# State space matrices of both halves built beside the first conditioning, both scans ahead of the readouts

## The chip, the cores and the metric

The kernel runs on one core of a Trainium2 chip. The metric is the device time of one execution in microseconds. TensorE (PE) multiplies matrices, VectorE (DVE), ScalarE (ACT) and GpSimd (POOL) do the rest, and SyncE (SP) issues the transfers. TensorE's clock has two levels, 1.2 and 2.4 GHz; the profile tells the granted level as a share of the upper one.

## What is computed

Two layers of a diffusion transformer with 512 latent tokens and 256 context tokens, D = 1024. Each layer mixes three things in parallel: windowed attention, a short convolution, and a bidirectional state space model (SSM) of 16 groups; then an MLP. The conditioning vector gives shifts, scales and gates. The context is computed in layer 0 only, beyond what layer 1 reads of it. The part that the change touches:

```python
mod = (c_act @ w_ada[l] + b_ada[l])[:, None, :]             # conditioning
q, k, v, cb, cc, cx, u = split_in_proj(h_lat @ w_in)
conv = cb * centred_conv3(cc * cx, conv_w)

lam_bar = jnp.exp(lam * dt)                                  # SSM, per direction and group
b_bar = ((lam_bar - 1) / lam)[..., None] * lax.complex(b_re, b_im)
# drive(t, d) = einsum('blgi,gpi->blgp', t, b_bar[d])
h_lat_f = diag_scan(lam_bar[0], drive(u, 0), h_ctx_f[:, -1], False)
h_lat_b = diag_scan(lam_bar[1], drive(u, 1), h_ctx_b[:, 0], True)
y = real(einsum('blgp,gip->blgi', hf, c_mat[0]) + einsum('blgp,gip->blgi', hb, c_mat[1])) + d_skip * t
g = gelu(y); out = g * sigmoid(g @ w_glu + b_glu)
```

## The kernel before

**Stages.** For each layer `block` runs `phase_w` (conditioning, SSM, convolution), `phase_a` (attention, the SSM's gate, output projection) and the MLP. In layer 0 `startup` comes first: the first half of the conditioning, the SSM's input projection u and the SSM matrices. The order on the engines is not that of the code: a scheduler places every instruction by dependences, buffers and its own times, and the code's order is what it starts from. Large products are made in three matmuls of high and low parts (L638 to L640). The conditioning that is left is spread over `phase_w` in slices (`step(sn[i])`), whose 32-row matmuls stand at L754 and whose weights SP loads in blocks of 512 KB (`w` from `w_ada`); ACT and DVE or POOL split each loaded weight into its two parts (L622, L623).

**The SSM.** Tokens are taken in chunks of 8, so that 96 chunks remain (64 of them latent). The 16 groups are worked in two halves of 8, and each in two directions. Its functions, by half:
- `ssm_mats`: input matrices `x` (DVE, L334 to L340), transposed on PE (L346) and copied to `xt`; small matmuls of 32 columns (L356 to L366, 24 of them) for the kernel strips, copied by ACT to `ssm_k` and stored to DRAM (`strips`). In the text these are the strip matmuls.
- `ssm_tm`: SP loads the strips back in Toeplitz form (`ssm_tr`, 512 KB) and ACT copies them into the order that the readout needs (`ssm_tm`, L568 through a helper).
- `ssm_out_mat`: the matrices `ssm_o` that lead from the state to the output (DVE, L442 to L447, 6 rows per direction).
- `ssm_scan`: the drive matmuls (L462), thirteen DVE instructions with the scan itself (L471 to L498, L484 the scan) per direction, which leave the states `ssm_s`; in layer 0 it calls `ssm_out_mat` for each direction.
- `ssm_read`: for each of four pairs of groups, one Toeplitz matmul per group (L519) and four of the states per group (L525), each on one half of PE's rows; the two groups of a pair go to two PSUM banks (`ps_s`). ACT and DVE evict each bank (L532 to L535) and SP stores it to `y_d`.

In layer 1 the matrices of both halves were made in layer 0's MLP and spilled to DRAM (`ssm_spill`); `ssm_fill` loads them.

**The convolution.** `conv("cc")`, `conv("cx")` and `conv("cb")` are projections into the PSUM tag `ps_m` of four banks; cc is evicted by ACT (L1127), cx and cb by DVE (L1129, L1142, L1144).

**Pools.** The tag A4 has four buffers of 4 KB per partition for `ssm_x`, `ssm_s` and `ssm_tr`; `ssm_tm` has one buffer of its own; the general pool `f4` has 19 buffers of 4 KB.

**Order in the code of `phase_w`.** Layer 0: matrices and Toeplitz matrix of half 0 come from `startup`; then scan 0, matrices of half 1, readout 0, conv cc, scan 1, Toeplitz 1, conv cx, readout 1, conv cb. Layer 1: scan 0, fill 1, scan 1, conv cc, readout 0, Toeplitz 1, conv cx, readout 1, conv cb. After that `phase_a` starts with the kv projection.

Of the kernel before, what the change touches and what calls it, by code (L numbers as in the profile page):

```python
# [7 lines left out]
F32 = mybir.dt.float32  # L8
# [7 lines left out]
P = 128  # L16
# [361 lines left out]

def ssm_tm(E, l, half):

    tr = E.mp.tile([P, 8, 8, 16], F32, name="ssm_tr", tag="A4", bufs=E.na4)
    tm = E.mp.tile([P, 8, 8, 16], F32, name="ssm_tm", tag="ssm_tm", bufs=1)
    st = E.strips[l]
    E.bdma(tr.rearrange("p t g i -> p t (g i)"),
           bass.AP(tensor=st.tensor, offset=st.offset + half * P, ap=[[256, P], [4096, 8], [1, P]]))
    E.copy(tm, tr.rearrange("p t g i -> p g t i"))
    return tm
# [27 lines left out]
def ssm_fill(E, half):  # L415
    U = {}
    for d in range(2):
        u = U[d] = Env()
        c0 = (2 + d) * 8 + half * 4
        u.cs = slice(c0, c0 + 4)  # L420
        u.xt = E.mp.tile([P, 2, 4, P], F32, name="ssm_xt", tag="B4", bufs=E.nb4)
        E.bdma(u.xt.rearrange("p q k c -> p (q k c)"), E.sp_x[half, d])
    for d in range(2):
        U[d].o = E.mp.tile([P, 2, 4, 8, 16], F32, name="ssm_o", tag="B4", bufs=E.nb4)
        E.bdma(U[d].o.rearrange("p q k t i -> p (q k t i)"), E.sp_o[half, d])
    return U


def ssm_out_mat(E, S, u, half, d):

    nc = E.nc
    V, G = nc.vector, nc.gpsimd
    cs = u.cs
    sl = slice(1, 9) if d == 0 else slice(8, 0, -1)
    pr, pi = bc(E.pw[:, 0, cs, sl], 3, 16), bc(E.pw[:, 1, cs, sl], 3, 16)
    pn = slice(half * 64, half * 64 + 64)
    cr = bc(S.c[:, 0, d, pn].rearrange("p (a i) -> p a i", i=16), 2, 8)
    ci = bc(S.c[:, 1, d, pn].rearrange("p (a i) -> p a i", i=16), 2, 8)
    o = E.mp.tile([P, 2, 4, 8, 16], F32, name="ssm_o", tag="B4", bufs=E.nb4)
    t1 = E.mp.tile([P, 4, 8, 16], F32, name="ssm_m", tag="T3", bufs=2)  # L440
    t2 = E.mp.tile([P, 4, 8, 16], F32, name="ssm_m", tag="T3", bufs=2)
    V.tensor_mul(o[:, 0], pr, cr)  # L442
    V.tensor_mul(t1, pi, ci)
    V.tensor_add(o[:, 0], o[:, 0], t1)
    V.tensor_mul(o[:, 1], pr, ci)
    V.tensor_mul(t2, pi, cr)
    V.tensor_sub(o[:, 1], o[:, 1], t2)  # L447
    u.o = o


def ssm_scan(E, S, U, u_t, l, half, lat_only):
    nc = E.nc
    V, G = nc.vector, nc.gpsimd
    sp = {}
    for d in range(2):
        u = U[d]
# [28 lines left out]
        s = E.mp.tile([P, 2, 4, NCH + CCH], F32, name="ssm_s", tag="A4", bufs=E.na4)  # L485
# [13 lines left out]
        if d == 1 and not lat_only:  # L499
            nc.scalar.copy(s[:, :, :, 0:CCH], s[:, :, :, NCH:NCH + CCH])  # L500
        sp[d] = s
        if l == 0:
            ssm_out_mat(E, S, u, half, d)
    return sp


# [455 lines left out]
def block(E, l, cols):  # L962
    tc, nc, a = E.tc, E.nc, E.a
    with psum_phase(E, f"w{l}", s=3, a=1, m=4) as E.pp, \
            tc.tile_pool(name=f"ssm{l}", bufs=1, reuse_waits="tile") as E.mp:
        E.ps, E.na4, E.nb4 = 's', 4, 4
        E.xa = lambda shape: E.mp.tile(shape, F32, name="ssm_x", tag="A4", bufs=E.na4)
        E.wpool = False
        if l == 0:
            cols = startup(E)  # L970
        st = phase_w(E, l, cols)
    with psum_phase(E, f"a{l}", m=2, t=2, q=2) as E.pp, \
            tc.tile_pool(name=f"att{l}", bufs=1, reuse_waits="tile") as E.ap:
        E.wpool = True
        phase_a(E, l, cols, st)
    with psum_phase(E, f"m{l}", m=3, a=1, q=2) as E.pp, \
            tc.tile_pool(name=f"mlp{l}", bufs=1, reuse_waits="tile") as E.g4p, \
            tc.tile_pool(name=f"prep{l}", bufs=1, reuse_waits="tile") as E.mp:
        E.ps, E.nb4 = 'a', 2
        E.xa = E.f4  # L980
        a2 = phase_post(E, l, st)
        return phase_mlp(E, l, a2)
# [7 lines left out]
def startup(E):  # L990
# [38 lines left out]
    S = E.S = ssm_load(E, a, 0)  # L1029
    S.tab = E.mp.tile([P, 2, 16, NCH], F32, name="ssm_tab", tag="ssm_tab", bufs=1)  # L1030
    ssm_table(E, 0, 16, S.tab)
    E.U0 = ssm_mats(E, E.S, 0, 0), ssm_tm(E, 0, 0)
    return cols


# [41 lines left out]
def phase_w(E, l, cols):  # L1077
    nc, a, tc = E.nc, E.a, E.tc
    V, G = nc.vector, nc.gpsimd
    both = l == 0  # L1080
# [11 lines left out]
    def step(n):  # L1092
        for _ in range(n):
            next(ada, None)
# [9 lines left out]
    S = E.S if l == 0 else Env()  # L1104
    if l == 1:
        S.tab = E.mp.tile([P, 2, 16, NCH], F32, name="ssm_tab", tag="ssm_tab", bufs=1)
        U0, t0 = ssm_fill(E, 0), ssm_tm(E, 1, 0)
        E.bdma(S.tab, E.sp_t)
    else:
        U0, t0 = E.U0  # L1110
    for h in range(2):
        E.bdma(u_t[h], E.u_d[h].rearrange("t i g c -> (t i) g c"))
    zs, mC = {}, {}
# [35 lines left out]
    step(sn[1])  # L1149
    wcx = blocks(E, wc, 4, 2, 8)  # L1150
    step(sn[2])
    s0 = ssm_scan(E, S, U0, u_t, l, 0, not both)
    if both:
        U1 = ssm_mats(E, S, 0, 1)
        ssm_read(E, U0, t0, s0, u_t, 0, y_d, not both)
        conv("cc", wcc)
        s1 = ssm_scan(E, S, U1, u_t, l, 1, not both)
    else:
        U1 = ssm_fill(E, 1)
        s1 = ssm_scan(E, S, U1, u_t, l, 1, not both)  # L1160
        conv("cc", wcc)
        ssm_read(E, U0, t0, s0, u_t, 0, y_d, not both)
    t1 = ssm_tm(E, l, 1)
    wcb = blocks(E, wc, 0, 2, 8)
    step(sn[3])
    conv("cx", wcx)
    ssm_read(E, U1, t1, s1, u_t, 1, y_d, not both)
    step(sn[4])
    conv("cb", wcb)
    st = Env()  # L1170
# [343 lines left out]
```

## Time and profile before

| | |
|---|---|
| median of 3 runs | 1687.18 us (1686.0 to 1687.56) |
| the profiled execution | 1684.55 us |
| its span in the profile | 1682.8 us |
| mean granted clock | 0.958 |
| PE busy | 1575.2 us, 94% |
| DVE busy | 891.2 us, 53% |
| ACT busy | 554.5 us, 33% |
| POOL busy | 302.9 us, 18% |

The span is the time from the first to the last instruction of the profiled execution, and its own time is 1.75 us longer. A row of busy time says how long an engine had an instruction in work, not how fast: at the lower clock PE is just as busy. A matmul of fp32 operands (L346, L462, L519, L525) shows as two records, so "x16" of these lines is 8 instructions.

### The profile page before, as it was taken

What the parts mean: (1) busy time and instruction counts of PE and PEld (TensorE: products, weight loads), DVE (VectorE), ACT (ScalarE), POOL (GpSimd) and SP (SyncE); (2) the same over time, 40 slices, a digit from 0 to 9 for tenths busy, and PEclk for the clock granted to TensorE, in tenths of its full rate; (3) what the DMA queues carried; (4) which work ended last, traced back from release to release, by engine and by line L of the source; (5) the groups of instructions that cost most, each with busy time, mean ns of one, the idle gap of its engine ahead of it and who ended that gap; (6) DMA issues with size and microseconds to landing.
All of it is one profiled execution on the core that took longest, in us unless ns stands there. A gap on an engine that the chain in (4) does not pass through costs nothing.

```text
span 1682.8 us, 22623 instructions
## 1 busy us (share of the span) xinstructions
PE 1575.2 (94%) x8872; PEld 1274.2 (76%) x8872; DVE 891.2 (53%) x1982; ACT 554.5 (33%) x1041; POOL 302.9 (18%) x231
## 2 busy tenths in 40 slices
PE   5999698999999999999999997999889899999997
PEld 2777576667888888868688875788667788888885
DVE  7882627766885463323333367643774733333335
ACT  5421125554523122121312344122554522322232
POOL 0000122002312111011111126012102322222222
PEclk9997699999999999999999998959999899999999
DMA  9564212004133222072621245822302232222223
GB/s 342 190 207 157 98 48 76 1 20 175 71 135 106 80 100 76 25 274 68 237 72 51 88 151 193 313 83 64 113 1 99 77 101 99 100 100 100 89 99 125
DMA packets 73274, 193.80 MB, mean 115 GB/s; under 512 B 15184, under 2 KB 25680, under 8 KB 73040
## 3 DMA queue, kind: packets, MB, share of 16 engines
q1 hardware_dynamic: 73168, 192.37, 33.1%
q8 instruction: 69, 1.13, 0.3%
q14 instruction: 37, 0.30, 0.1%
HBM read 172.15 MB, written 20.19 MB: 114 GB/s over the span
## 4 chain that ended last, share of the span: by engine, by line
PE 78%; DVE 13%; ACT 4%; DMA 2%; issue 2%; POOL 1%; DVEq 0%; SPq 0%; ACTq 0%; POOLq 0%
PE ps_m L638 14%; PE ps_m L639 14%; PE ps_m L640 14%; PE ps_q L639 8%; PE ps_q L638 8%; PE ps_q L640 8%; PE ps_s L525 2%; PE ps_a L754 2%; ACT p L873 2%; DVE p L865 1%; PE ps_t L898 1%; DVE p L878 1%; PE ps_s L519 1%; DVE w L623 1%; PE ps_t L891 1%
## 5 line engine op out<-in xcount | busy, mean ns | idle before, releaser
L622 ACT CAST w<-w 128x1024 fp32r<-128x1024 f32 x172 | 178.8, 1049 | 477.2 <-PE ps_q L639 312.8
L623 POOL TENSOR_TENSOR w<-w 128x1024 fp32r<-128x1024 f32 x79 | 193.2, 2445 | 780.1 <-ACT w L622 343.5
L638 PE MATMUL ps_q<-w,f 128*128 128x512 f32 x640 | 247.3, 391 | 3.4 <-DVE g L1466 2.6
L639 PE MATMUL ps_q<-w,f 128*128 128x512 f32 x640 | 248.5, 390 | 1.9 <-DVE w L623 1.1
L640 PE MATMUL ps_q<-w,f 128*128 128x512 f32 x640 | 246.7, 389 | 0.0
L623 DVE TENSOR_TENSOR w<-w 128x1024 fp32r<-128x1024 f32 x93 | 117.8, 1266 | 149.7 <-ACT w L622 125.3
L638 PE MATMUL ps_m<-g,w 128*128 128x256 f32 (+1 forms) x544 | 178.8, 333 | 2.3 <-DVE g L711 1.8
L639 PE MATMUL ps_m<-g,w 128*128 128x256 f32 (+1 forms) x544 | 179.7, 332 | 0.0
L640 PE MATMUL ps_m<-g,w 128*128 128x256 f32 (+1 forms) x544 | 177.9, 331 | 0.0
L639 PE MATMUL ps_m<-f,w 128*128 128x512 f32 (+1 forms) x464 | 171.6, 371 | 0.5 <-POOL f L714 0.3
L640 PE MATMUL ps_m<-f,w 128*128 128x512 f32 (+1 forms) x464 | 171.2, 370 | 0.0
L638 PE MATMUL ps_m<-f,w 128*128 128x512 f32 (+1 forms) x464 | 169.5, 369 | 0.3 <-DVE f L1071 0.3
L1472 DVE TENSOR_TENSOR g<-g,ps_q 128x1024 f32<-128x1024 f32 x60 | 73.3, 1221 | 178.6 <-PE ps_q L640 178.6
L638 PEld LDWEIGHTS ps_q<-w,f 128*128 128x128 f32 x640 | 119.8, 188 | 29.9 <-DVE g L1466 3.9
L639 PEld LDWEIGHTS ps_q<-w,f 128*128 128x128 f32 x640 | 120.2, 188 | 27.5 <-DVE w L623 2.0
L640 PEld LDWEIGHTS ps_q<-w,f 128*128 128x128 f32 x640 | 120.2, 188 | 24.7
L638 PE MATMUL ps_m<-w,f 128*128 128x512 f32 (+1 forms) x336 | 124.6, 374 | 6.8 <-DVE p L918 4.0
L640 PE MATMUL ps_m<-w,f 128*128 128x512 f32 (+1 forms) x336 | 124.2, 371 | 0.0
L639 PE MATMUL ps_m<-w,f 128*128 128x512 f32 (+1 forms) x336 | 123.0, 368 | 0.0
L1395 DVE SCALAR_TENSOR_TENSOR relu<-ps_m,relu 128x512 f32<-128x512 f32 (+1 forms) x104 | 58.7, 566 | 120.0 <-ACT relu L1394 119.8
L638 PEld LDWEIGHTS ps_m<-g,w 128*128 128x128 f32 x544 | 104.0, 193 | 15.7 <-issue 2.5
L639 PEld LDWEIGHTS ps_m<-g,w 128*128 128x128 f32 x544 | 104.9, 193 | 11.6 <-issue 1.6
(284 smaller groups left out, 2578.7 us busy)
## 6 DMA issues: line engine op xcount, KB each, us to landing
w<-in_w_ada SPq DMA_DIRECT2D x88, 512.0 KB
w<-in_w_mlp_in SPq DMA_DIRECT2D x64, 512.0 KB
w<-in_w_mlp_out SPq DMA_DIRECT2D x64, 512.0 KB
w<-in_w_out SPq DMA_DIRECT2D x16, 512.0 KB
w<-in_w_conv SPq DMA_DIRECT2D x12, 512.0 KB
h_d<-g SPq DMA_DIRECT2D x12, 512.0 KB
w<-in_w_q SPq DMA_DIRECT2D x8, 512.0 KB
f<-h_d SPq DMA_DIRECT2D x8, 512.0 KB
```

Source lines behind the costliest of these rows:

```text
L519: nc.tensor.matmul(out(g), tm[:, g8].rearrange("p t i -> p (t i)"), u_t[half][:, g8, lo:NCH], start=True, stop=False, skip_group_check=True)
L525: nc.tensor.matmul(out(g), U[d].o[rows, q, k].rearrange("p t i -> p (t i)"), sp[d][rows, q, k, lo:NCH], start=False, stop=d == 1 and q == ...
L622: nc.scalar.copy(hi, raw)
L623: (nc.gpsimd if turn % 2 and E.wpool else nc.vector).tensor_sub(lo, raw, hi.bitcast(F32))
L638: nc.tensor.matmul(out, lh, rh, start=first, stop=False)
L639: nc.tensor.matmul(out, lh, rl, start=False, stop=False)
L640: nc.tensor.matmul(out, ll, rh, start=False, stop=last)
L754: nc.tensor.matmul(pa[32 * b:32 * b + 32, k * 256:(k + 1) * 256], E.cT[:, kc], raw[k][:, b * 256:(b + 1) * 256], start=kc == 0 and k == 0, ...
L865: V.tensor_tensor_reduce(out=p[i][:, :nk * P], in0=pq[:, l0:768], in1=E.mask[:, moff:moff + nk].rearrange("p a b -> p (a b)"), scale=0.125 ...
L873: nc.scalar.activation(p[i][:, :nk * P], p[i][:, :nk * P], AF.Exp, bias=nm[:, i:i + 1], accum_out=sm[:, i:i + 1])
L1395: V.scalar_tensor_tensor(out=s, in0=pt, scalar=0.0, in1=s, op0=OP.max, op1=OP.mult)
L1472: V.tensor_add(facc[t], facc[t], pq)
```

## The change

Both Toeplitz tiles come from the pool `f4`; A4 has five buffers in place of four. `startup` makes the matrices of both halves, and no Toeplitz matrix. `ssm_scan` no longer makes the out matrices. In `phase_w` Toeplitz 0 comes ahead of scan 0, and the code's order is then: scan 0, out matrices of half 0 (layer 0) or fill 1 (layer 1), scan 1, readout 0, Toeplitz 1, out matrices of half 1 (layer 0), conv cc, readout 1, conv cx, conv cb.

```diff
@@ -378,8 +378,7 @@
 
 def ssm_tm(E, l, half):
 
-    tr = E.mp.tile([P, 8, 8, 16], F32, name="ssm_tr", tag="A4", bufs=E.na4)
-    tm = E.mp.tile([P, 8, 8, 16], F32, name="ssm_tm", tag="ssm_tm", bufs=1)
+    tr, tm = (E.f4([P, 8, 8, 16]) for _ in range(2))
     st = E.strips[l]
     E.bdma(tr.rearrange("p t g i -> p t (g i)"),
            bass.AP(tensor=st.tensor, offset=st.offset + half * P, ap=[[256, P], [4096, 8], [1, P]]))
@@ -499,8 +498,6 @@
         if d == 1 and not lat_only:
             nc.scalar.copy(s[:, :, :, 0:CCH], s[:, :, :, NCH:NCH + CCH])
         sp[d] = s
-        if l == 0:
-            ssm_out_mat(E, S, u, half, d)
     return sp
 
 
@@ -963,7 +960,7 @@
     tc, nc, a = E.tc, E.nc, E.a
     with psum_phase(E, f"w{l}", s=3, a=1, m=4) as E.pp, \
             tc.tile_pool(name=f"ssm{l}", bufs=1, reuse_waits="tile") as E.mp:
-        E.ps, E.na4, E.nb4 = 's', 4, 4
+        E.ps, E.na4, E.nb4 = 's', 5, 4
         E.xa = lambda shape: E.mp.tile(shape, F32, name="ssm_x", tag="A4", bufs=E.na4)
         E.wpool = False
         if l == 0:
@@ -1029,7 +1026,7 @@
     S = E.S = ssm_load(E, a, 0)
     S.tab = E.mp.tile([P, 2, 16, NCH], F32, name="ssm_tab", tag="ssm_tab", bufs=1)
     ssm_table(E, 0, 16, S.tab)
-    E.U0 = ssm_mats(E, E.S, 0, 0), ssm_tm(E, 0, 0)
+    E.U = [ssm_mats(E, S, 0, h) for h in range(2)]
     return cols
 
 
@@ -1104,10 +1101,10 @@
     S = E.S if l == 0 else Env()
     if l == 1:
         S.tab = E.mp.tile([P, 2, 16, NCH], F32, name="ssm_tab", tag="ssm_tab", bufs=1)
-        U0, t0 = ssm_fill(E, 0), ssm_tm(E, 1, 0)
+        U = [ssm_fill(E, 0)]
         E.bdma(S.tab, E.sp_t)
     else:
-        U0, t0 = E.U0
+        U = E.U
     for h in range(2):
         E.bdma(u_t[h], E.u_d[h].rearrange("t i g c -> (t i) g c"))
     zs, mC = {}, {}
@@ -1149,22 +1146,24 @@
     step(sn[1])
     wcx = blocks(E, wc, 4, 2, 8)
     step(sn[2])
-    s0 = ssm_scan(E, S, U0, u_t, l, 0, not both)
+    tms = [ssm_tm(E, l, 0)]
+    sp = [ssm_scan(E, S, U[0], u_t, l, 0, not both)]
     if both:
-        U1 = ssm_mats(E, S, 0, 1)
-        ssm_read(E, U0, t0, s0, u_t, 0, y_d, not both)
-        conv("cc", wcc)
-        s1 = ssm_scan(E, S, U1, u_t, l, 1, not both)
+        for d in range(2):
+            ssm_out_mat(E, S, U[0][d], 0, d)
     else:
-        U1 = ssm_fill(E, 1)
-        s1 = ssm_scan(E, S, U1, u_t, l, 1, not both)
-        conv("cc", wcc)
-        ssm_read(E, U0, t0, s0, u_t, 0, y_d, not both)
-    t1 = ssm_tm(E, l, 1)
+        U.append(ssm_fill(E, 1))
+    sp.append(ssm_scan(E, S, U[1], u_t, l, 1, not both))
+    ssm_read(E, U[0], tms[0], sp[0], u_t, 0, y_d, not both)
+    tms.append(ssm_tm(E, l, 1))
+    if both:
+        for d in range(2):
+            ssm_out_mat(E, S, U[1][d], 1, d)
+    conv("cc", wcc)
     wcb = blocks(E, wc, 0, 2, 8)
     step(sn[3])
+    ssm_read(E, U[1], tms[1], sp[1], u_t, 1, y_d, not both)
     conv("cx", wcx)
-    ssm_read(E, U1, t1, s1, u_t, 1, y_d, not both)
     step(sn[4])
     conv("cb", wcb)
     st = Env()
```

Above line 500 the new kernel's line numbers are lower by 1, and from 501 on by 3: L525 becomes L522, L1127 becomes L1124.

What the scheduler makes of it, at three places of layer 0. On ACT, near the end of the strip matmuls, before: `f4_1309` and `f4_1363` are conv cc's tiles, `ssm_k` the strips, `ssm_tm_994` the Toeplitz matrix of half 0.

```order
L1127 COPY f4_1309<-ps_m_1337 128x256
L568 COPY ssm_xt_925<-ps_s_926 128x512
L568 COPY ssm_xt_925<-ps_s_932 128x512
L1127 COPY f4_1363<-ps_m_1365 128x512
L568 COPY ssm_xt_947<-ps_s_948 128x512
L568 COPY ssm_xt_947<-ps_s_954 128x512
L568 COPY ssm_k_977<-ps_s_960 128x128
L568 COPY ssm_k_990<-ps_s_981 128x128
L622 CAST w_1520<-w_1516 128x1024
```

The same place on ACT now: `f4_1155` and `f4_1387` are the Toeplitz matrices of half 0 and half 1, `f4_1386` the load of the second, `f4_1408` and `f4_1462` conv cc's tiles.

```order
L565 COPY f4_1155<-f4_1154 128x1024
L619 CAST w_1524<-w_1518 128x1024
L565 COPY ssm_k_1060<-ps_s_1043 128x128
L565 COPY ssm_k_1073<-ps_s_1064 128x128
L565 COPY f4_1387<-f4_1386 128x1024
L1124 COPY f4_1408<-ps_m_1410 128x512
L1124 COPY f4_1408<-ps_m_1436 128x256
L1124 COPY f4_1462<-ps_m_1464 128x512
L1124 COPY f4_1462<-ps_m_1490 128x256
```

The four evictions of conv cc now stand behind the second half's strips and its Toeplitz copy, before they stood ahead of them.

On PE, in the first readout of layer 0, before: `ps_s_1253` and `ps_s_1254` are its two banks, `ssm_s` the states, `ssm_o` the out matrices.

```order
L519 MATMUL ps_s_1253<-u_t0_998,ssm_tm_994 128x96
L519 MATMUL ps_s_1254<-u_t0_998,ssm_tm_994 128x96
L525 MATMUL ps_s_1253<-ssm_s_1106,ssm_o_1113 128x96
L525 MATMUL ps_s_1254<-ssm_s_1106,ssm_o_1113 128x96
L525 MATMUL ps_s_1253<-ssm_s_1106,ssm_o_1113 128x96
L525 MATMUL ps_s_1254<-ssm_s_1106,ssm_o_1113 128x96
L525 MATMUL ps_s_1253<-ssm_s_1153,ssm_o_1161 128x96
L525 MATMUL ps_s_1254<-ssm_s_1153,ssm_o_1161 128x96
```

The first readout now: `ps_s_1330` is its first bank.

```order
L516 MATMUL ps_s_1330<-u_t0_1077,f4_1155 128x96
L522 MATMUL ps_s_1330<-ssm_s_1189,ssm_o_1235 128x96 x2
L522 MATMUL ps_s_1330<-ssm_s_1227,ssm_o_1244 128x96 x2
L516 MATMUL ps_s_1330<-u_t0_1077,f4_1155 128x96
L522 MATMUL ps_s_1330<-ssm_s_1189,ssm_o_1235 128x96 x2
L522 MATMUL ps_s_1330<-ssm_s_1227,ssm_o_1244 128x96 x2
```

The groups of the two banks took turns before; now the four groups of one bank follow each other, and those of the other (`ps_s_1331`) come after 4 transposes (L763) and 31 matmuls of projections (24 of 256 columns, 7 of 512).

On DVE, at the end of `phase_w` in layer 0, before: the second scan's last direction (`ssm_z_1482`) and its out matrix (`ssm_o_1503`), then the evictions of the second readout (L533, L535).

```order
L484 SCALAR_TENSOR_TENSOR ssm_z_1482<-ssm_rz_1490,ssm_z_1482 128x384 x2
L495 TENSOR_TENSOR ssm_s_1495<-ssm_z_1482,ssm_tab_850 128x8x95
L496 TENSOR_TENSOR ssm_zt_1496<-ssm_z_1482,ssm_tab_850 128x8x95
L443 TENSOR_TENSOR ssm_m_1504<-ssm_pw_84,ssm_c_835 128x512
L497 TENSOR_TENSOR ssm_s_1495<-ssm_s_1495,ssm_zt_1496 128x4x95
L498 TENSOR_TENSOR ssm_s_1495<-ssm_s_1495,ssm_zt_1496 128x4x95
L444 TENSOR_TENSOR ssm_o_1503<-ssm_o_1503,ssm_m_1504 128x512
L446 TENSOR_TENSOR ssm_m_1505<-ssm_pw_84,ssm_c_835 128x512
L447 TENSOR_TENSOR ssm_o_1503<-ssm_o_1503,ssm_m_1505 128x512
L533 SCALAR_TENSOR_TENSOR ssm_y2_1774<-ssm_y2_1774,ps_s_1732 128x384
```

The end of the second half's out matrices on DVE now: `ssm_o_1390` and `ssm_o_1399` are those of its two directions, `ssm_y2_1379` and `ssm_gl_1380` belong to the first readout's second bank, `ssm_y2_1656` to the second readout.

```order
L530 SCALAR_TENSOR_TENSOR ssm_y2_1379<-ssm_y2_1379,ps_s_1331 128x384
L442 TENSOR_TENSOR ssm_m_1400<-ssm_pw_84,ssm_c_835 128x512
L446 TENSOR_TENSOR ssm_o_1390<-ssm_o_1390,ssm_m_1392 128x512
L443 TENSOR_TENSOR ssm_o_1399<-ssm_o_1399,ssm_m_1400 128x512
L445 TENSOR_TENSOR ssm_m_1401<-ssm_pw_84,ssm_c_835 128x512
L532 SCALAR_TENSOR_TENSOR ssm_gl_1380<-ssm_y2_1379,ps_s_1331 128x384
L446 TENSOR_TENSOR ssm_o_1399<-ssm_o_1399,ssm_m_1401 128x512
L530 SCALAR_TENSOR_TENSOR ssm_y2_1656<-ssm_y2_1656,ps_s_1614 128x384
```

The second half's scan and out matrices, which came after the first readout and most of the convolution, are now done beside the first readout.

## Rows read from the trace of the kernel before

**Rows 1.** The page's busy line: busy us, share of the span, instructions.

```profile
PE 1575.2 (94%) x8872; PEld 1274.2 (76%) x8872; DVE 891.2 (53%) x1982; ACT 554.5 (33%) x1041; POOL 302.9 (18%) x231
```

**Rows 2.** Windows of layer 0: length, busy us by engine, PE clock, DMA share, GB/s.

```profile
80.00:90.00 10.00, 10.00 (x101) 7.37 (x101) 1.68 (x3) 3.19 (x9) 0.62 (x3) 0.83 0.60 234
...
130.00:140.00 10.00, 10.00 (x84) 7.39 (x83) 0.28 (x1) 2.02 (x4) 0.11 (x1) 0.89 0.62 202
140.00:150.00 10.00, 10.00 (x54) 8.80 (x55) 0.00 (x0) 0.27 (x1) 0.11 (x1) 0.50 0.07 25
150.00:160.00 10.00, 9.86 (x96) 7.01 (x93) 3.52 (x6) 1.96 (x3) 0.00 (x0) 0.59 0.35 106
160.00:170.00 10.00, 9.77 (x123) 6.73 (x124) 7.52 (x14) 1.63 (x3) 0.10 (x1) 1.00 0.98 336
170.00:180.00 10.00, 4.90 (x30) 3.98 (x28) 10.00 (x15) 4.59 (x5) 5.24 (x2) 0.77 0.37 125
180.00:190.00 10.00, 1.46 (x7) 0.97 (x6) 9.85 (x19) 0.41 (x1) 0.30 (x2) 0.50 0.28 106
```

**Rows 3.** Waits of PE from 72 to 202: us in total, times, longest.

```profile
PE ps_s L525 <- DVE ssm_o L444: 11.5, 2, 7.0
PE ps_s L525 <- DVE ssm_o L447: 2.0, 2, 1.6
PE ps_s L519 <- DVE ssm_z L473: 0.6, 1, 0.6
```

**Rows 4.** Chain of waits, 138 to 159: start, us, what (first readout, Toeplitz load).

```profile
148.47 1.10 PE ps_s L519 x4
149.57 1.96 PE ps_s L525 x16
...
153.82 4.10 DMA ssm_tr<-strips
```

**Rows 5.** Chain of waits in layer 1's first readout, groups one by one.

```profile
1094.34 1.03 PE ps_s L525 x8
1095.37 0.36 PE ps_s L519 x2
...
1099.12 0.62 PE ps_s L519 x2
1099.74 1.90 PE ps_s L525 x8
```

**Rows 6.** Windows behind the two readouts: length, PE busy us, clock, DMA share, GB/s.

```profile
154.60:158.10 3.50, 3.50 (x36) 0.50 0.54 157
...
201.20:206.00 4.80, 4.80 (x23) 0.50 0.16 41
```

**Rows 7.** Timeline of ACT: start, us, instruction, idle before it and what ended that.

```profile
69.96 0.60 ACT L1127 COPY f<-ps_m 128x512 f32<-128x512 f32 x1
...
92.44 1.05 ACT L568 COPY ssm_tm<-ssm_tr 128x1024 f32<-128x1024 f32 x1 [1.53 <-DMA ssm_tr<-strips]
```

**Rows 8.** Prices on PE from the chain, in four stretches of 64 to 97.

```profile
64.39 0.23 PE ps_m L639
...
69.50 0.12 PE ps_m L638
...
78.97 0.56 PE ps_a L754 x4
...
86.03 0.22 PE ps_s L358 x2
...
95.32 0.81 PE ps_s L462 x16
```

**Rows 9.** Chain of waits at the operand split, 60 to 62.

```profile
59.88 0.60 DVE ssm_x L338
```

**Rows 10.** Waits of PE in layer 1, 1090 to 1140.

```profile
PE ps_s L519 <- ACT ssm_tm L568: 3.3, 1, 3.3
```

**Rows 11.** VectorE's groups from 155 to 193: busy us, mean ns, idle before.

```profile
L623 DVE TENSOR_TENSOR w<-w 128x1024 fp32r<-128x1024 f32 x2 | 4.1, 2058 | 0.0
```

## The prediction

> **What bounds the kernel now.** I read the page's busy line first: PE has 94% of the span [rows 1], so a gain can only come from stretches where PE waits, or where it works at the lower clock. The windows of 10 us over layer 0's projections come next [rows 2]: PE is full up to 170, has 4.90 and 1.46 busy us in the next two windows, and the granted clock is 0.50 from 140 to 150 and from 180 to 190. That is the place of the change. The list of waits says who is late there [rows 3]: PE waits for VectorE's `ssm_o` rows, 11.5 + 2.0 us, and 0.6 us for `ssm_z`, 14.1 in all. The chain of waits around 140 to 160 shows what else is slow: the first readout runs at the low clock, a pair of groups costing 1.10 + 1.96 = 3.06 us, and the second half's Toeplitz load takes 4.10 us [rows 4]. In layer 1 the same views show readouts group by group [rows 5], and one wait of 3.3 us for `ssm_tm` [rows 10]. The rest, some 1500 us, the change leaves alone but for small reorderings.
>
> The profiled execution took 1684.55 us (span 1682.8), the median of the three runs is 1687.18; I sum against the profiled one and add the 2.63 between them at the end. Below, "low" is a granted clock of 0.50, 1.2 GHz, and "full" is 1.00, 2.4 GHz.
>
> **The idle time (layer 0): -14.1 us.** Before, the second half's scan and out matrices stand on VectorE behind the conv rows, so PE gets to the second readout before its operands. After, both scans stand in front, and the last `ssm_o` row is row 381 of VectorE, ahead of the second readout's first eviction. Does it fit? From 160 to 190 VectorE is busy 7.52 + 10.00 + 9.85 = 27.4 us; from 130 to 160 it is idle for 9.72 + 10.00 + 6.48 = 26.2 us [rows 2]. Of the 27.4, 4.1 are two weight splits [rows 11] that don't move, and conv and conditioning rows stand there too; so at most 23.3 move into 26.2, an estimate of 22 with those rows taken off: it fits with about 4 us to spare. So all three waits of [rows 3] go, and what is late next is not VectorE but ACT (below). If the 4 us are overdrawn, the overdraft comes back as the same wait, us for us.
>
> **The readouts (layer 0): -1.0 us.** Before, both readouts run in pairs over two PSUM banks at the low clock: 8 pairs x 3.06 = 24.5 us [rows 4]. After, the first readout is issued bank by bank, four groups in a row, then projections, then the other four; the second has its first pair scattered among conditioning matmuls and three pairs in a row. A group by itself costs 0.36 + 1.03 = 1.39 us at full clock and 0.62 + 1.90 = 2.52 at low [rows 5], so alone it saves nothing: two groups at low clock cost 5.04 against 3.06 for a pair. What it can gain is the clock: before a serial readout in layer 1 the clock is full, and the first two groups there still run at full. I take the same here: of each four, 2.1 at 1.39 and 1.9 at 2.52, 7.7 us, twice, 15.4. For the second readout: the scattered pair at full 1.8, then pairs at half of 3.06 for the first 2.9 us and at 3.06 after that, 6.3; 8.1. Sum 23.5 against 24.5. Bounds: everything at full 8 x 1.39 + 1.8 + 3 x 1.53 = 17.5, everything at low 8 x 2.52 + 4 x 3.06 = 32.4; so -7.0 to +7.9. I take the middle since the rows show the first part at full and the rest low.
>
> **Low clock on other work (layer 0): +0.4 us.** The clock stays low behind each stretch of small or half-row matmuls: 3.5 us behind the first readout, 4.8 us behind the second [rows 6], and about 3.4 us each with the two halves' small strip matmuls (clock 0.83 from 80 to 90, 0.89 from 130 to 140 and 0.50 until the readout starts at 141.2) [rows 2]. Work there takes twice its time, so half of each is lost: 1.75 + 2.4 + 2 x 1.7 = 7.6 us. After, there are three tails of readouts (two banks of the first, and the second) at 2.1, and the dip with the first half's strip matmuls, 1.7: 8.0. The dip behind the second half's is inside the next term.
>
> **A new wait of PE for ACT: +3.0 us.** The second half's strips, their load and the Toeplitz copy now come before the conv. On ACT the copy of the second Toeplitz matrix (`f4_1387`) stands ahead of the four evictions of conv cc; PE's first cx matmul needs one of these four PSUM banks. So PE there waits for: strip matmuls end, strips stored, Toeplitz loaded, copied, evicted. Before, the last strip matmul ends at 86.25 [rows 8] and the copy starts at 92.44 and takes 1.05; an eviction is 0.60 [rows 7]: 6.2 + 1.05 + 0.6 = 7.8 us. PE's work in between is 40 drive matmuls (8 cost 0.81) and 6 of 256 columns (0.12 each) [rows 8]: 4.8 us at full clock. The rest, 3.0, is wait (or low clock in its place, the sum is the same). Bounds: 0 if the load is quick, and 1 us more for each us that store or load is later than before.
> The load of 512 KB takes 4.10 us where it is waited for [rows 4]. The Trainium skill ("DMA: Bandwidth & Descriptors", the section on the anatomy of one DMA) fits 2.0 us + bytes / 436e3 for the path through GpSimd, an estimate of 3.2 us for 512 KB; by it the wait and the sum would be 0.9 us less. This kernel's transfers are on the hardware queue, and the row is longer, so the row decides.
>
> **Startup: +1.2 us.** Two VectorE rows of the second half's matrices (L334 and L338, 0.60 each) now stand ahead of the operand split L714 for which PE waits already (VectorE is in the chain of waits there [rows 9]), so PE stops 1.2 us longer there. The other rows of these matrices run before 90, where VectorE has 1.68 us of 10 busy [rows 2]. Between 0, if the scheduler's rows are ready earlier than before, and 1.2. The larger pool (five tiles in place of four) and the two 4 KB tiles add no instruction; SP gets the second half's three transfers ahead of the `w_ada` loads, a few us of a queue that runs ahead.
>
> **Layer 1: -1.3 us.** The wait of 3.3 us for the Toeplitz copy goes [rows 10], since the copy is issued earlier. The second readout has six groups alone and one pair, before four and two pairs: at low clock 2 x 2.52 in place of 3.06 [rows 4, 5], +2.0.
>
> **The sum.** -14.1 - 1.0 + 0.4 + 3.0 + 1.2 = -10.5 in layer 0, -1.3 in layer 1: -11.8. 1684.55 - 11.8 = 1672.8; on the scale of the median **1675.4 us**.
>
> **The rivals.**
> *The clock stays up.* VectorE's new order takes the gap of 20 us out of PE's row, and the readouts are split by projections at full width, so the clock may not fall in them. Then they cost 17.5 (6.0 less) and the three tails go too (6.3): 1663 to 1669. Against it: every readout of the trace falls to 0.50 within itself [rows 2, 5]. 14%.
> *The wait moves to ACT or stays with VectorE.* If strips or load are late beside the `w_ada` traffic, or the 4 us of room on VectorE are overdrawn, each us late is one us on PE. Six to ten us late: 1681 to 1686. For it: a chain through two transfers, and VectorE full; against: the first half's chain runs beside the same traffic and takes the 7.8 us. 15%.
> *Slower: the clock stays low from the first serial readout to the kv projection.* Serial groups fill half of PE's rows, two banks of them with only about 5 us of projections between. Behind the readout's start lie some 21.5 us of other matmuls (48 of 256 columns at 0.12, 24 of 512 at 0.23, 64 of conditioning at 0.14 [rows 8], and 8 transposes, put at 0.15) and the readouts; my forecast gives them 21.5 + 23.5 + 6.3 = 51.3, all at low clock they take 43.0 + 32.4 = 75.4. That is 24.1 more, 1700 at the end, and slower than before by 0.2% from 63% of it, that is if most of the projections between also run low. For it: at low clock serial groups cost 1.6 times a pair [rows 4, 5]. Against: behind the first readout before, the clock is up again after 3.5 us [rows 6]. 1691 to 1700, 12%.
>
> **How the numbers follow.** Forecast 59%, in 1670 to 1681; the rivals as above. 0.2% is 3.4 us, about what a measurement of this kernel can tell from no change: faster is below 1683.8, slower above 1690.5. Faster: nearly all of the forecast (58), the first rival (14), half of the second (7): 79%, less 1 for what I have not seen. No change: the rest of the second and a little of the forecast, 9%. Slower 13%. The range 1663 to 1687 leaves out the slow rival and the ends of the others.
>
> **What would show it.** In the profile after: the two `ssm_o` waits of 11.5 us gone; a wait of PE for ACT's L1124 of about 3 us near 105; the first readout in two blocks of 6 to 8 us near 135 to 160 with the clock falling inside each; the kv projection starting near 191 in place of 201; PE waiting 1.2 us more near 61; layer 1's 3.3 us wait for the Toeplitz copy gone. I am wrong if PE still waits for `ssm_o`, if the ACT wait is over 6 us, or if the clock between the two blocks of the first readout stays at 0.50.

## The result and the profile after

The changed kernel takes 1669.09 us (median of four runs, 1665.55 to 1670.84), the kernel before 1686.59 beside it: a ratio of 0.9895, 95% interval 0.9875 to 0.9914. That is 17.5 us less; 11.8 were forecast (1675.4 us), and the time lies in the range. The profiled execution took 1670.84 us, the slowest of the four, and its span is 1669.1 against 1682.8: in the two traces the gain is 13.7 us. The rest of the 17.5 lies between the profiled executions and the medians.

The page's busy line and the windows of layer 0's projections, as in [rows 1] and [rows 2] (length, busy us by engine, PE's clock, DMA share, GB/s):

```profile
PE 1575.2 (94%) x8872; PEld 1273.2 (76%) x8872; DVE 896.0 (54%) x1982; ACT 553.7 (33%) x1041; POOL 301.8 (18%) x231
```

```profile
140.00:150.00 10.00, 10.00 (x63) 8.73 (x63) 7.32 (x12) 1.11 (x2) 0.00 (x0) 0.70 0.12 43
150.00:160.00 10.00, 10.00 (x58) 9.22 (x58) 7.48 (x15) 0.93 (x2) 0.10 (x1) 0.78 0.33 107
...
170.00:180.00 10.00, 10.00 (x91) 6.77 (x89) 1.16 (x2) 0.00 (x0) 0.00 (x0) 1.00 1.03 389
180.00:190.00 10.00, 9.11 (x103) 7.22 (x101) 6.42 (x10) 5.48 (x8) 2.42 (x1) 1.00 0.52 161
```

PE's busy time is the same to the tenth, so the busy line says nothing about the gain. The windows do: the hole of 4.90 and 1.46 busy us in the last two windows of [rows 2] is gone, and VectorE, which was idle from 140 to 150, now has 7.32 us of work there. PE's waits from 72 to 205, as in [rows 3] (us, times, longest):

```profile
PE ps_m L635 <- DVE mod L766: 1.2, 1, 1.2
PE ps_m L635 <- ACT f L1124: 0.8, 1, 0.8
```

The 14.1 us for `ssm_o` and `ssm_z` are gone; the wait for the conditioning slice (`mod`) just ahead of the kv projection is new. That projection starts at 190.32, before at 201.1. PE's timeline over the first readout's first bank, as in [rows 5] (start, us, instruction):

```profile
140.92 0.46 PE L516 MATMUL ps_s<-u_t,f 128*128 128x96 f32 x2
141.31 1.13 PE L522 MATMUL ps_s<-ssm_s,ssm_o 64*128 64x96 f32 x8
142.37 0.46 PE L516 MATMUL ps_s<-u_t,f 128*128 128x96 f32 x2
142.76 1.13 PE L522 MATMUL ps_s<-ssm_s,ssm_o 64*128 64x96 f32 x8
143.82 0.51 PE L516 MATMUL ps_s<-u_t,f 128*128 128x96 f32 x2
144.27 2.02 PE L522 MATMUL ps_s<-ssm_s,ssm_o 64*128 64x96 f32 x8
146.22 0.74 PE L516 MATMUL ps_s<-u_t,f 128*128 128x96 f32 x2
146.89 2.02 PE L522 MATMUL ps_s<-ssm_s,ssm_o 64*128 64x96 f32 x8
```

Two groups at the full clock, the fall, two at the low one. To see where the time goes I also followed single matmuls through both timelines. Early in layer 0's `phase_a`, one that starts at 241.2 before is 13.0 us earlier now; the end of the span is 13.7 earlier. So layer 0, up to the end of its `phase_w`, makes nearly all of it. PE's windows from 40 us to just ahead of that matmul, before and after:

```profile
40.00:238.74 198.74, 182.91 (x1317) 0.86 0.46 149
40.00:225.78 185.78, 181.18 (x1318) 0.92 0.49 159
```

PE stands idle for 4.6 us there in place of 15.8, so 11.2 of the 13.0 us are waits; the other 1.8 are in the speed of its work.

### The profile page after: what moved, and what is told of

It reads as the page before. It is cut to its first block, busy times and chain, and to the rows that moved or that the text cites. A ratio compares the mean times of both kernels' runs of the same rounds, so it can differ in the third digit from the quotient of the medians.

```text
span 1669.1 us, 22624 instructions
## 1 busy us (share of the span) xinstructions
PE 1575.2 (94%) x8872; PEld 1273.2 (76%) x8872; DVE 896.0 (54%) x1982; ACT 553.7 (33%) x1041; POOL 301.8 (18%) x231
## 3 DMA queue, kind: packets, MB, share of 16 engines
q8 instruction: 69, 1.13, 0.3%
## 4 chain that ended last, share of the span: by engine, by line
PE 79%; DVE 12%; ACT 5%; issue 2%; DMA 1%; POOL 1%; SPq 0%; DVEq 0%; ACTq 0%; POOLq 0%
PE ps_m L635 14%; PE ps_m L636 14%; PE ps_m L637 14%; PE ps_q L636 8%; PE ps_q L635 8%; PE ps_q L637 8%; PE ps_a L751 3%; PE ps_s L522 2%; ACT p L870 2%; PE ps_t L895 2%; DVE p L862 1%; DVE p L875 1%; PE ps_s L516 1%; PE ps_t L888 1%; DVE rs L583 1%
## 5 line engine op out<-in xcount | busy, mean ns | idle before, releaser
L636 PEld LDWEIGHTS ps_m<-g,w 128*128 128x128 f32 x544 | 104.0, 191 | 11.8 <-issue 1.6
```

The source lines that it names most:

```text
L636: nc.tensor.matmul(out, lh, rl, start=False, stop=False)
```

## Experiments

The first theory was the prediction's: the new order of the calls lifts the second half's scan ahead of the convolution, so PE's wait goes. The rival: the early matrices do it. Since the answers crossed, the three parts of the change (matrices early, calls in new order, new tiles) were run in all eight combinations; besides, four runs on PSUM banks and two on single terms. One cell is not pure: order_old is made from the changed kernel, so its first Toeplitz call stands in `phase_w` and its out matrices behind the scan, in mats_only and tiles_only they stand as before. Each shift below is that of the matmul at 241.2 of the profile before, so layer 0 alone and of one profiled execution; waits and clock are those of PE from 72 and 70 to 205.

| kernel | early matrices | new order | new tiles | median us | ratio, 95% interval | PE waits us | mean clock | layer 0 shift us |
|---|---|---|---|---|---|---|---|---|
| before | | | | 1686.59 | | 14.4 | 0.80 | |
| mats_only | x | | | 1688.13 | 1.0013 (1.0002 to 1.0025) | 21.1 | 0.84 | +3.8 |
| order_only | | x | | 1671.12 | 0.9902 (0.9879 to 0.9925) | 4.7 | 0.85 | -7.5 |
| tiles_only | | | x | 1675.60 | 0.9946 (0.9931 to 0.9960) | 11.1 | 0.86 | -6.2 |
| order_old | x | | x | 1667.05 | 0.9882 (0.9860 to 0.9904) | 3.1 | 0.92 | -17.0 |
| mats_late | | x | x | 1683.48 | 0.9982 (0.9964 to 1.0001) | 14.8 | 0.81 | +3.5 |
| tiles_old | x | x | | 1652.54 | 0.9784 (0.9757 to 0.9811) | 0.3 | 0.95 | -22.6 |
| the change | x | x | x | 1669.09 | 0.9895 (0.9875 to 0.9914) | 2.0 | 0.89 | -13.0 |

**order_old**: the calls of `phase_w` in the old order, the rest as changed.

```diff
-    sp.append(ssm_scan(E, S, U[1], u_t, l, 1, not both))
     ssm_read(E, U[0], tms[0], sp[0], u_t, 0, y_d, not both)
-    tms.append(ssm_tm(E, l, 1))
...
+    conv("cc", wcc)
+    sp.append(ssm_scan(E, S, U[1], u_t, l, 1, not both))
...
+    tms.append(ssm_tm(E, l, 1))
+    conv("cx", wcx)
+    ssm_read(E, U[1], tms[1], sp[1], u_t, 1, y_d, not both)
```

> The changed kernel with the order of the SSM calls in phase_w put back (scan 0, readout 0, conv cc, scan 1, Toeplitz 1, conv cx, readout 1); the matrices of both halves stay in startup and the new tiles stay. Theory A (the order of the scans makes the gain, since the second scan's VectorE rows get ahead of the convolution): PE waits for ssm_o or ssm_s of half 1 again, 8 to 14 us, time 1679 to 1686. Rival B (the early matrices make it: 12 VectorE rows and 24 strip matmuls leave the late stretch): no such wait over 3 us, time 1666 to 1674.

Measured 1667.05 us, within rival B's bounds, with one wait for `ssm_o`:

```profile
PE ps_s L522 <- DVE ssm_o L446: 2.8, 1, 2.8
PE ps_a L763 <- DVE t L760: 0.3, 1, 0.3
```

The old order is as fast as the new one here, so the order is not necessary. Three pairs of its first readout follow each other again, at the full clock (1.00 from 137 to 142).

**mats_late**: the matrices of half 1 in `phase_w` again.

```diff
-    E.U = [ssm_mats(E, S, 0, h) for h in range(2)]
+    E.U = [ssm_mats(E, S, 0, 0)]
...
             ssm_out_mat(E, S, U[0][d], 0, d)
+        U.append(ssm_mats(E, S, 0, 1))
```

> The changed kernel with the matrices of half 1 built in phase_w again, behind the first scan and its out matrices; both scans still ahead of the readouts. Theory A: the order is enough, VectorE still gets to the second half's states before the second readout, time 1666 to 1675, and the 1.2 us at startup are back (operand split wait near 61 at 0.2). Rival B: without the early matrices VectorE is late again for the second half, PE waits 8 us or more for ssm_o, time 1680 to 1687.

Measured 1683.48 us: rival B's time, but not by its mechanism. There is no wait for `ssm_o` at all; PE waits for conditioning weights:

```profile
PE ps_a L751 <- DMA w<-in_w_ada: 14.0, 8, 3.6
PE ps_a L763 <- DVE t L760: 0.8, 1, 0.8
```

In its order 32 conditioning matmuls stand in a row ahead of the second half's matrices, and PE waits eight times for their loads between 96 and 119. The startup wait is back at 0.2. So this run does not show that early matrices are needed for VectorE; without them the scheduler pulls other work forward, and that work isn't ready.

**mats_only**: the kernel before with the early matrices alone.

```diff
     E.U0 = ssm_mats(E, E.S, 0, 0), ssm_tm(E, 0, 0)
+    E.U1 = ssm_mats(E, E.S, 0, 1)
...
-        U1 = ssm_mats(E, S, 0, 1)
+        U1 = E.U1
```

> The kernel before with one part of the change: the matrices of both halves built in startup; tiles, order of the calls and out matrices as before. Theory B (early matrices are the gain, since order_old kept it with the old order): 1667 to 1674, PE's waits for ssm_o under 4 us in layer 0. Rival C (the tiles are needed as well: with four A4 buffers and the Toeplitz load among them the second half's states wait for a buffer, so its scan stays late on VectorE): waits of 6 us or more at the second readout, 1678 to 1688.

Measured 1688.13 us; theory B falls, and the waits are those of rival C:

```profile
PE ps_s L525 <- DVE ssm_o L444: 17.9, 2, 11.4
PE ps_s L462 <- DVE ssm_gl L535: 1.3, 1, 1.3
```

With the strip matmuls of half 1 done by 114, a quarter of its drive matmuls runs at 138, but the others still run at 163 to 172, behind the first readout, and the scan behind them; the conv, which went on for 4 us behind the last of them before, is done by then. Early matrices help only if the drive matmuls can run early too. That a buffer holds the states back, as rival C had it, is not shown.

**tiles_only**: the kernel before with the two tiles from `f4` and five A4 buffers.

```diff
-    tr = E.mp.tile([P, 8, 8, 16], F32, name="ssm_tr", tag="A4", bufs=E.na4)
-    tm = E.mp.tile([P, 8, 8, 16], F32, name="ssm_tm", tag="ssm_tm", bufs=1)
+    tr, tm = (E.f4([P, 8, 8, 16]) for _ in range(2))
...
-        E.ps, E.na4, E.nb4 = 's', 4, 4
+        E.ps, E.na4, E.nb4 = 's', 5, 4
```

> The kernel before with the other part of the change: the Toeplitz tiles from the general pool and five A4 buffers, matrices of half 1 and order of the calls as before. Theory B: the second half's strip and drive matmuls stay behind the convolution, so its scan and the wait for ssm_o stay, 1680 to 1688. Rival C: a fifth buffer alone lets them run early, 1667 to 1675.

Measured 1675.60 us, between the two, at the rival's end. The waits are shorter, not gone:

```profile
PE ps_s L524 <- DVE ssm_o L446: 5.2, 1, 5.2
PE ps_s L461 <- DVE ssm_gl L534: 2.0, 1, 2.0
PE ps_m L637 <- ACT f L1126: 1.8, 1, 1.8
```

**toep_f4_four**: the same with four A4 buffers.

```diff
-        E.ps, E.na4, E.nb4 = 's', 5, 4
+        E.ps, E.na4, E.nb4 = 's', 4, 4
```

> The kernel before with the Toeplitz tiles from the general pool but four A4 buffers, so only half of the tile edit. Tells which half of tiles_only's 11 us it is: if the Toeplitz load leaving A4 and the second copy having its own tile do it, 1674 to 1678, with no wait for the Toeplitz copy in layer 1 (3.3 us before); if the fifth A4 buffer does it (transposes of half 1 some 6 us earlier), 1681 to 1686.

Measured 1673.16 us, a ratio of 0.9907 (0.9887 to 0.9928), a layer 0 shift of -9.6 us, and no wait for the Toeplitz copy in layer 1. The time is just below the first range. So the Toeplitz tiles' move to the general pool makes the gain of tiles_only, and the fifth buffer adds nothing to it. Which of the two tiles does it was not run.

**order_only**: the kernel before with the new order of the calls and the out matrices outside the scan (the change without its edits of `ssm_tm` and `na4` and without the early matrices; the first Toeplitz call stands in `phase_w`, as in the change).

```diff
+    sp = [ssm_scan(E, S, U[0], u_t, l, 0, not both)]
...
+        U.append(ssm_mats(E, S, 0, 1))
...
+    sp.append(ssm_scan(E, S, U[1], u_t, l, 1, not both))
+    ssm_read(E, U[0], tms[0], sp[0], u_t, 0, y_d, not both)
```

> The kernel before with the third part of the change alone: both scans ahead of the readouts, out matrices outside the scan; matrices of half 1 in phase_w behind the first scan, tiles as before. The first theory, on which the prediction stood (the order lifts the second half's scan ahead of the convolution): ssm_o waits under 3 us, 1668 to 1676. If the order does little without early matrices and tiles: the strip and drive matmuls of half 1 stay behind the convolution, 1680 to 1690.

Measured 1671.12 us, within the first theory's time, but with 4.2 us of the wait left where it asked for under 3:

```profile
PE ps_s L523 <- DVE ssm_o L447: 4.2, 1, 4.2
PE ps_m L636 <- DVE ssm_gl L533: 0.5, 1, 0.5
```

So by the median the order is enough for as much as the whole change gives, and (order_old) not necessary. In layer 0 it gives only 7.5 of the 13.0 us; another 6.3 of its profiled execution lie behind it.

**tiles_old**: the change with the tiles of before.

```diff
-    tr, tm = (E.f4([P, 8, 8, 16]) for _ in range(2))
+    tr = E.mp.tile([P, 8, 8, 16], F32, name="ssm_tr", tag="A4", bufs=E.na4)
+    tm = E.mp.tile([P, 8, 8, 16], F32, name="ssm_tm", tag="ssm_tm", bufs=1)
...
-        E.ps, E.na4, E.nb4 = 's', 5, 4
+        E.ps, E.na4, E.nb4 = 's', 4, 4
```

> The changed kernel with the tiles of before (Toeplitz load in A4, its copy in a buffer of its own, four A4 buffers); early matrices and new order stay. If early matrices need the new tiles in either order, as they did in the old one (mats_only 1688 against 1667 with the tiles): 1678 to 1688, with a wait of PE of 6 us or more in layer 0 or in front of the second Toeplitz matrix in layer 1. If the new order replaces the tiles: 1667 to 1673.

Measured 1652.54 us, outside both expectations and by its median the fastest of all: 0.9784 of before, and 16.6 us under the whole change by the medians. Its four executions lie from 1647.02 to 1656.54, and the profiled one is the slowest; against the change's it has 14.3 us less, 9.7 in layer 0 and 4.7 behind it. So the tile edit, which gains 11 us on the kernel before, costs 16.6 beside the other two. In layer 0 PE waits for almost nothing and has a clock of 0.95 in place of 0.89. The window from 70 to 205 of the kernel before (length, PE busy, clock, DMA share, GB/s):

```profile
70.00:205.00 135.00, 120.44 (x923) 0.80 0.52 172
```

of the change:

```profile
70.00:205.00 135.00, 132.98 (x1038) 0.89 0.53 180
```

of order_only:

```profile
70.00:205.00 135.00, 130.26 (x977) 0.85 0.55 180
```

and of tiles_old:

```profile
70.00:205.00 135.00, 134.66 (x1098) 0.95 0.57 188
```

A mean of 0.95 is 13.5 us at the low clock (0.05 x 2 x 135), 0.89 is 29.7, 0.80 is 54. What the tile edit does here can be read in part. In the change a third pair of VectorE rows (L334, L338) stands ahead of the operand split L711, so PE waits 1.4 us near 61, 0.2 before; with the tiles of before two pairs stand ahead of the split and the wait is 0.2. That it is the fifth buffer that lets the third pair in is argued: five buffers with late matrices (mats_late) have two pairs. The other waits are 1.7 us longer in the stretch (2.0 against 0.3). And the second Toeplitz load goes out at 103.91 with the new tiles, at 153.67 with the old, where nothing of PE's waits for it. The clock makes the rest: 16 us less at the low one, worth up to 8. Together up to 11, for 9.7 measured in layer 0 (22.6 less 13.0). Why the clock stayed up at the second half's strip and drive matmuls in tiles_old (1.00 from 96.2 to 106.4) and not in the change is open; the rows around them are nearly the same. Behind layer 0 the readouts of layer 1 make most of the difference: they take 25.0 us of PE's time in place of 30.6, the second of them in pairs again, while a wait of 2.9 us for the Toeplitz copy is back. The edit was not run by halves in this place, so whether the fifth buffer or the move of the tiles costs the 16.6 is open.

**tm_late**: the second Toeplitz call behind conv cc.

```diff
-    tms.append(ssm_tm(E, l, 1))
...
     conv("cc", wcc)
+    tms.append(ssm_tm(E, l, 1))
```

> The changed kernel with the second Toeplitz load and copy issued behind conv cc in both layers, so that ACT's four conv cc evictions need not stand behind its copy. If the wait for ACT costs what the sum said (3.0 us with the low clock in it), PE goes from the last strip matmul of half 1 to the first cx matmul in 5 to 6 us in place of 7.7 and the time is 1666 to 1667.5. If only the 0.8 us of true wait is to be had, because the rest is drive matmuls at the low clock, the time is 1668 to 1669.5 and the stretch is 6.5 to 7 us.

Measured 1671.25 us (1665.65 to 1673.01), ratio 0.9900 (0.9873 to 0.9926): no gain, and outside both expectations. The wait for ACT is gone, and the stretch from the last strip matmul to the first cx matmul is as long as with it. The window of that stretch in the change (length, PE busy, clock, DMA share, GB/s):

```profile
102.00:109.60 7.60, 6.84 (x86) 0.70 0.28 80
```

and in tm_late:

```profile
102.60:110.20 7.60, 7.60 (x87) 0.62 0.28 80
```

The drive matmuls fill the time at the low clock. In tiles_old the stretch with the same drive matmuls takes 5.2 us at 1.00. So the price there was the clock's, not ACT's.

**ps4**: the change with four PSUM banks for the SSM and three for the projections.

```diff
-    with psum_phase(E, f"w{l}", s=3, a=1, m=4) as E.pp, \
+    with psum_phase(E, f"w{l}", s=4, a=1, m=3) as E.pp, \
```

> The changed kernel with four PSUM banks for the SSM and three for the projections (before: three and four). In its order the first readout runs in pairs over two banks again, since a second bank is free. Theory A (groups by themselves cost 1.4 us against 0.8 to 1.5 for one of a pair): the first readout takes 7 to 12 us in place of 14.3, time 1662 to 1668. Rival (the fourth projection bank is worth more than the pairs): PE waits 3 us or more for the evictions of ps_m, time 1670 to 1676.

Measured 1655.53 us, ratio 0.9814 (0.9793 to 0.9836); theory A's mechanism, and 6.5 us under its range. The first readout in PE's timeline:

```profile
135.83 0.68 PE L522 MATMUL ps_s<-ssm_s,ssm_o 64*128 64x96 f32 x4
...
138.51 1.14 PE L522 MATMUL ps_s<-ssm_s,ssm_o 64*128 64x96 f32 x16
...
141.25 0.69 PE L516 MATMUL ps_s<-u_t,f 128*128 128x96 f32 x4
141.87 1.14 PE L522 MATMUL ps_s<-ssm_s,ssm_o 64*128 64x96 f32 x16
```

It takes 7.5 us at the full clock throughout, against 8.0 + 6.3 in the change. So the bank-by-bank order of the change comes from the new order of the calls with three banks in the PSUM pool: a scan takes two banks per direction, and with three only one is left for the readout. (order_old has pairs with three.) Layer 0's shift is -17.5, 4.5 better than the change, and layer 1 gives the rest.

**before_ps4**: the same one-line edit on the kernel before.

> The kernel before with four PSUM banks for the SSM and three for the projections, nothing else. Its first readout is in pairs already, so if the bank pays by pairs in place of serial groups, layer 0 gains nothing and only layer 1 can: 1676 to 1686. If the fourth bank pays by itself (drive matmuls and readouts of the second half no longer wait for a bank): 1665 to 1675.

Measured 1660.97 us, ratio 0.9862 (0.9844 to 0.9880). PE's waits from 70 to 205:

```profile
PE ps_s L462 <- DVE ssm_gl L535: 2.1, 2, 1.3
PE ps_a L754 <- DMA w<-in_w_ada: 0.8, 1, 0.8
PE ps_a L754 <- PE ps_s L462: 0.4, 1, 0.4
```

The `ssm_o` wait is gone with neither the order of the calls nor the matrices touched. The second half's drive matmuls now run at 140 to 150, before at 154 to 168. The time is 4 us under the second expectation's range, but its reason is not what the trace shows: the drive matmuls wait 2.1 us for evictions of the readout (`ssm_gl`), before 0.3. They follow right behind the first readout, as before; that starts at 133.0 in place of 141.0, and it runs at the full clock. Its first and last pair:

```profile
133.61 1.14 PE L525 MATMUL ps_s<-ssm_s,ssm_o 64*128 64x96 f32 x16
...
138.65 1.14 PE L525 MATMUL ps_s<-ssm_s,ssm_o 64*128 64x96 f32 x16
```

The two readouts of layer 0 together take 13.9 us of PE's time in place of 27.3. So of the shift of -18.5 us the larger part is the clock in the readouts. Why it stays up there, behind the same strip matmuls, is open.

**order_old_ps4** and **ps5**: order_old with four banks for the SSM, and the change with five and two for the projections.

> The kernel order_old (old order of the calls, early matrices, new tiles) with four PSUM banks for the SSM and three for the projections. Layer 0's readouts are in pairs in order_old already, so if the bank pays by pairs, layer 0 gains 0 to 3 us here and layer 1, which has serial groups in order_old, 8 to 10: 1655 to 1659. If the order of the calls matters once the readouts are in pairs, it is apart from the same edit on the changed kernel (1655.5) by over 4 us.

> The changed kernel with five PSUM banks for the SSM and two for the projections. If two banks are enough for projections (an eviction of 0.6 us against 3 to 6 us of matmuls per bank) and layer 1's second readout, which waits for ssm_s, gains by more banks for its drive matmuls: 1648 to 1655. If projections stall on two banks: waits for ps_m over 4 us, 1658 to 1668.

Measured 1657.23 us (0.9833, 0.9818 to 0.9847) and 1657.07 us (0.9811, 0.9792 to 0.9831). Once there are four banks, the old and the new order are equal within their ranges (1657.2 against 1655.5), and a fifth bank brings nothing more. Against order_old the fourth bank gives 3.8 us in layer 0 and 9.2 behind it, nearly as expected. ps5 lies between its two ranges: in layer 0's `phase_w` no wait of a projection is over 1.6 us, but ahead of it 6.8 us for conditioning weights are new.

## Why the prediction was right, and where it was not

**The sum.** -13.7 us between the two traces against -11.8: layer 0 -13.0 against -10.5, the rest -0.7 against -1.3. In layer 0 the waits give -11.2 (forecast -14.1, +1.2 and what of ACT's 3.0 is wait), the readouts -5.3 (forecast -1.0) and other work some +3.5 (forecast +0.4 and the rest of ACT's 3.0). So the mechanism was right and the mis-sized term is that of the readouts. By the medians the miss is 6.3 us, not 1.9: the 2.63 us were added to come from a profiled execution below its median, and that of the change is 1.75 above its own.

**The idle time.** The 14.1 us went as forecast, and VectorE's rows fit into its idle stretch as worked out: no wait for `ssm_o` is left. Not forecast: 1.2 us for the conditioning slice. The reason given was only one of several. The prediction said that the wait goes because both scans stand in front. order_only shows that this is enough for 9.7 of the 14.4 us of waits, order_old that it goes as far without it (3.1 left), before_ps4 that one PSUM bank does it too. What they share is that the second half's drive matmuls are over earlier. The last of them starts at 167.6 before and 172.2 in mats_only, with 13.5 and 18.4 us of waits for `ssm_o`; at 157.4 in tiles_only (5.2 us), 152.3 in order_old (2.8), 149.5 in before_ps4 (none), 148.5 in order_only (4.2) and 140.7 in the change (none). Who may start early is decided by buffers and banks as much as by the order of the calls.

**The readouts.** First bank 8.0 us (forecast 7.7), second bank 6.3 from 156.4 to 162.7 (7.7), since the clock was full again before it and fell late (mean 0.88). The second readout's pairs ran at the full clock, 1.7 us each from 176.7 to 181.7, where 6.3 for the three were put. With 2.7 us for the scattered first pair of the second, the readouts take 22.0 us where 23.5 were put: right within 2 us. The time before was put too low: eight pairs at 3.06 are 24.5, and PE's timeline has 27.3, namely 13.5 for the first readout, 9.2 for three pairs of the second and 4.6 for the scattered matmuls of its first pair. The first two of these as windows of before:

```profile
141.00:154.50 13.50, 13.50 (x81) 0.50 0.03 9
191.97:201.13 9.16, 9.16 (x63) 0.50 0.01 2
```

So the term is -5.3 us where -1.0 was put. What the prediction left out is why the order was bank by bank; ps4 prices that: 14.3 us against 7.5.

The Trainium skill ("TensorEngine Tiling (Array Packing)", Gotcha 1) says that different row tiles write to different PSUM banks and cannot access one bank at the same time. The rows fit it: 8 records alone take 1.13 us, 16 in pairs over two banks 1.14. No readout here has both halves of the rows at work on one bank.

**Low clock on other work.** Forecast +0.4, by tails. The tails are there (5.5 us at 0.51 behind the first bank, 148.9 to 154.4). A second tail of 5.3 us at 0.50 stands behind the second bank (162.7 to 168.0), none behind the second readout. So the term's size holds. But the whole stretch spent some 30 us at the low clock in place of 54, by the mean of the window. Of PE's work the readouts have 6.9 us at the low clock in place of 26.9; the idle hole had some 11 more. From 175.3 to 206.0 before, the clock was 0.50 over the hole and the second readout behind it, and with the wait that readout's low clock went too. That is the clearest miss: the prediction priced the wait and the low clock behind it apart, and only the wait in full.

**The wait for ACT.** From the last strip matmul to the first cx matmul 7.8 us were forecast and 7.7 measured (101.96 to 109.65), in the chain of waits as said:

```profile
102.27 1.58 DMA strips<-ssm_k
103.85 0.02 SPq L566
103.88 0.03 issue
103.91 4.13 DMA f<-strips
108.04 0.02 issue
108.06 1.05 ACT f L565
109.11 0.49 ACT f L1124
```

0.8 of it is true wait. The rest is drive matmuls at the low clock, and tm_late shows that they take as long without the wait. The load took 4.13 us. The estimate of 3.2 us by the Trainium skill ("DMA: Bandwidth & Descriptors", the section on the anatomy of one DMA) is for the path through GpSimd; it is too short for this load on the hardware queue, which it was not fitted to.

**Startup.** Forecast +1.2, measured +1.2 (1.4 against 0.2):

```profile
62.64 0.50 PE L636 MATMUL ps_m<-f,w 128*128 128x512 f32 x1 [1.37 <-DVE f L711]
```

The two rows ahead of the split are those named, but the early matrices alone don't put them there: with the tiles of before (tiles_old) the wait is 0.2, and with the new tiles and late matrices (mats_late) it is 0.2 too.

**The tiles, priced at nothing.** "The larger pool (five tiles in place of four) and the two 4 KB tiles add no instruction". They add none, but with other buffers the scheduler places other work early. The sum did not suffer by it, since it was worked out from the order that the scheduler had made of the whole change; what it could not tell is what each part is worth. The tile edit moves the time by -11.0 us on the kernel before, by -21.1 beside the early matrices (where the first Toeplitz call and the out matrices move as well), by +12.4 beside the new order and by +16.6 beside both (by medians). The three parts do not add.

**Layer 1.** Its wait of 3.3 us went as forecast; a wait of 0.8 us for `ssm_s` is new. Of the 13.7 us, 0.7 lie behind layer 0's `phase_w`, against 1.3. In the other runs with three banks that remainder lies between +2.8 (mats_only, 6.6 in all less 3.8) and -6.3 us (order_only, 13.8 less 7.5), and kernels with the same code in layer 1 differ there: mats_only is 2.8 over before, mats_late (-2.1) 1.4 under the change. A term of one us can't be told there.

**The rivals.** The clock that stays up came true in part (second readout). The wait that moves to ACT did not, and the clock that stays low did not: after the first bank it was up again by 155. The argument against the first, that every readout falls to 0.50 within itself, misread layer 0 of the kernel before: there the clock was at 0.50 before the readouts began (from 137.8 and from 175.3 on). Not seen at all: that a version with less of the change would be faster.

## What to carry to other kernels

When a scheduler places the work, the buffers of its tiles (how many, from which pool) are as strong an edit as the order of calls: try each part of a combined change alone and each part left out, since here one third of the change cost nearly as much as the whole gained. Where PE waits for a chain that starts with its own matmuls, look at the PSUM banks too; one bank moved from one pool to another gave 25 us on the kernel before. A wait can also cost the low clock of the work behind it (before, 0.50 from 175.3 to 206.0), and a wait that lies beside low-clock matmuls may cost nothing (tm_late).

## What the runs showed of the hardware

Half-row matmuls in pairs over two PSUM banks at the full clock take the time of half as many alone (1.14 us for 16 records, 1.13 for 8). In pairs of 96 columns the granted clock stayed at 1.00 for a whole first readout (7.5 us in ps4, 6.7 in before_ps4); groups alone lost it 3.2 and 4.9 us into the two banks of the change. It is not the pairs alone that keep it: it fell 1.3 us into the pairs of 96 columns of tiles_only's first readout, which stand right behind strip matmuls, and of order_old's second, right behind a wait of 2.8 us. In layer 1, pairs of 64 columns kept it for 6.5 us in before_ps4 and lost it 4.4 us into the readout in ps4:

```profile
1077.72 1.11 PE L522 MATMUL ps_s<-ssm_s,ssm_o 64*128 64x64 f32 x16
1078.76 0.71 PE L516 MATMUL ps_s<-u_t,f 128*128 128x64 f32 x4
1079.40 1.97 PE L522 MATMUL ps_s<-ssm_s,ssm_o 64*128 64x64 f32 x16
```
